# A change to a two-layer hybrid backbone on one core: where the weights of the passage between its layers, a block of adaLN, and the last head's sigmoids stand in the order of work

## The chip, the core and the metric

The kernel runs on one core of a Trainium2 chip. The time is the device time in microseconds of one execution of the program; several executions give a median. Engines are called TensorE (PE in rows), VectorE (DVE), ScalarE (ACT), GpSimd (POOL) and SyncE (SP, which issues the loads of the weights).

## What is computed

Two layers over 256 context and 512 latent tokens of width 1024. Each layer: RMS norm, a shift and scale from adaLN (a small matrix product with the condition c), a mixer of inner width 2048, and a residual with a gate from adaLN.

```python
# layer 0: HGRN2, 16 heads, forward and backward; layer 1: RG-LRU, 8 heads of 256, forward and backward
h = rms(x) * (1 + scale) + shift              # scale, shift, gate = adaLN(c)
# layer 0
q, v, zf, zb, g = split(h @ w_in)
o = scan(q, 1-f, log f, v)  both ways         # chunked; f = lb + (1-lb) sigmoid(z)
x += gate * ((rms(o) * silu(g)) @ w_out)
# layer 1
xb, g = split(h @ w_in); xb = conv4(xb)
r, i = sigmoid(xb @ w_a + b_a), sigmoid(xb @ w_x + b_x)
a = exp(-8 r softplus(-lam)); u = sqrt(1 - a*a) * (i * xb)
y = scan(a, u) both ways                      # h_t = a_t h_(t-1) + u_t
x += gate * ((y * silu(g)) @ w_out)
out = rms(x) for the latent tokens
```

## The kernel before

Products are kept in float32 precision with float32r operands: each matrix is held as a rounded part (hi) and a remainder (lo), and each product takes three matmuls, hi by hi, hi by lo and lo by hi (`mm3`, lines 307 to 313). A weight comes as one load of 512 KB into one of three raw buffers; ACT copies it to hi (line 129), DVE subtracts to lo (line 130). The class `Weights` keeps them in the order of first use: `get` loads and splits the weight asked for, loads some further ones, and, where `presplit` is set, splits the next one as well. `slots` gives a weight other buffers than the standard ones, and adaLN's weights are used raw. Where several instructions are ready, the framework orders each engine's queue by the order of the program and by priority; `high_priority(urgent)` puts the splits ahead of what stands around them. Each engine then runs its queue in order.

Layer 0 runs head by head. `hgrn(h)` holds seven levels of score products (`lv`), whose operands `kt`, `qt` and `QQ` come from ACT and DVE, then the states and the outputs. `head_in(h+1)`, the next head's input products, is interleaved as filler, and `out_item` adds the output product of two or three heads to x. adaLN's blocks for layer 1 run beside heads 9 to 14 as `side`: four weights of four loads each into `ada` (line 230), a copy `blk`, a transposing product `adat` and two adds (lines 235 to 246).

The passage (lines 722 to 743) is: the output product of head 15 (`o`, context tiles d = 0 to 7, then latent ones), with x updated by DVE (line 405), squares by ACT (`sq`) and their sums in three accumulators, one of which POOL adds (`acc`, line 289); after the last tile of a segment the norm's statistics, `rstd_of`: products `msh` with a vector of ones, the root `rh` on ACT, and `rbh`, its broadcast over the partitions by TensorE; then `hchunk`, which makes layer 1's input `h_hi` and `h_lo` through `scr`; and with each piece the first products of layer 1, `rc` for the context and `rl` for the latent tokens, of three weights.

Layer 1 runs 8 heads. `mixer(j)` first makes the gates (`gt`, evacuated by ACT's sigmoids into R and G), then T, A and R by tanh and exp, roots, DVE's scans and `yh`, `yl`; the next head's input products and the output product of the head before (`ro`) are the filler. ACT's functions come in sets that each need a table load, so `after` chains sigmoids, exps and roots. For the last head (j = 7) no next head is there: `held` adds the output products of heads 5 and 6 in eight accumulators, and the end is the output product of head 7, the sum of squares and the final norm.

## Time and profile before

| | us |
|---|---|
| median of 3 runs (lowest, highest) | 1578.45 (1577.46, 1580.52) |
| the profiled execution | 1582.77 |
| its span, first to last instruction | 1581.0 |
| TensorE busy | 1531.9 (97%) |
| DVE busy | 1194.8 (76%) |
| ACT busy | 902.2 (57%) |
| POOL busy | 11.5 (1%) |
| mean granted clock of TensorE | 0.986 |

The times of instructions below are those of the profiled execution, in microseconds from the start of its span. A busy TensorE is not one at its peak, since it also counts as busy at the lower clock. Releasers ("<-") are inferred from semaphores: the instruction that ended the wait.

### The profile page before, as it was taken

To read this page: it belongs to the slowest core of one execution; us is meant where nothing else is said; L and a number is where in the kernel's file an instruction comes from. 1 tells how busy PE (TensorE), PEld (TensorE's weight loads), DVE (VectorE), ACT (ScalarE), POOL (GpSimd) and SP (SyncE) were. 2 spreads that over 40 slices of the span, in tenths; PEclk is the share of its full clock that TensorE was granted. 3 is DMA by queue.
4 is the path that set the end of the run, shared out by engine and by line. 5 is a ranking of instruction groups with operands and counts; after the bars stand their busy time and mean duration, and the time that the engine had idled before them with its cause. 6 is when DMAs were issued, how large, how long until landed. Compare 5 with 4: busy or idle time off the path is not lost.

```text
span 1581.0 us, 33998 instructions
## 1 busy us (share of the span) xinstructions
PE 1531.9 (97%) x14740; PEld 1432.8 (91%) x14740; DVE 1194.8 (76%) x1848; ACT 902.2 (57%) x1422; POOL 11.5 (1%) x16
## 2 busy tenths in 40 slices
PE   5999999999999999999999999998999999999996
PEld 3899999999999999999999999987888888988985
DVE  4767678768867868867876776786758887897877
ACT  4554554555554554554545555654577577667783
POOL 0000000000000000000000000001000000000001
PEclk9999999999999999999999999998999999999998
DMA  8231211110211211223222131202212213222211
GB/s 327 81 121 55 95 55 41 55 55 28 82 41 42 68 42 54 81 68 98 69 92 80 55 111 65 95 15 67 67 54 81 81 54 94 80 68 73 75 40 53
DMA packets 33861, 116.80 MB, mean 74 GB/s; under 512 B 3632, under 2 KB 6064, under 8 KB 33712
## 3 DMA queue, kind: packets, MB, share of 16 engines
q1 hardware_dynamic: 32192, 113.26, 22.3%
q8 instruction: 116, 1.90, 0.5%
q10 hardware_dynamic: 1520, 1.37, 0.3%
q14 instruction: 33, 0.27, 0.0%
HBM read 112.52 MB, written 2.10 MB: 72 GB/s over the span
## 4 chain that ended last, share of the span: by engine, by line
PE 88%; DVE 5%; ACT 5%; issue 1%; DMA 1%; POOL 0%; POOLq 0%; ACTq 0%; DVEq 0%; SPq 0%
PE in L311 12%; PE in L312 11%; PE in L313 11%; PE v L381 9%; PE lv L460 4%; PE o L565 4%; PE r L313 3%; PE r L312 3%; PE r L311 3%; PE o L311 3%; PE o L313 3%; PE o L312 3%; PE gt L311 2%; PE gt L312 2%; PE gt L313 2%; PE U L533 2%
## 5 line engine op out<-in xcount | busy, mean ns | idle before, releaser
L311 PE MATMUL in<-h_hi,hi 128*128 128x384 f32 x1024 | 350.2, 343 | 3.4 <-ACT h_hi L304 2.7
L312 PE MATMUL in<-h_lo,hi 128*128 128x384 f32 x1024 | 345.7, 338 | 0.7 <-DVE h_lo L305 0.7
L313 PE MATMUL in<-h_hi,lo 128*128 128x384 f32 x1024 | 344.8, 337 | 0.0
L130 DVE TENSOR_TENSOR lo<-raw,hi 128x1024 fp32r<-128x1024 f32 x160 | 195.0, 1220 | 90.6 <-ACT hi L129 90.4
L129 ACT ACTIVATE hi<-raw 128x1024 fp32r<-128x1024 f32 x160 | 167.9, 1057 | 122.4 <-PE in L312 49.9
L311 PEld LDWEIGHTS in<-h_hi,hi 128*128 128x128 f32 x1024 | 192.8, 189 | 16.8 <-issue 9.9
L312 PEld LDWEIGHTS in<-h_lo,hi 128*128 128x128 f32 x1024 | 193.1, 189 | 3.0 <-issue 1.6
L313 PEld LDWEIGHTS in<-h_hi,lo 128*128 128x128 f32 x1024 | 192.8, 188 | 1.2 <-issue 0.8
L509 DVE TENSOR_TENSOR QQ<-QQ,T 128x768 f32<-128x768 f32 x112 | 117.6, 1050 | 20.7 <-ACT qt L491 20.5
L416 ACT ACTIVATE kt<-KK 128x768 f32<-128x768 f32 x112 | 102.5, 915 | 40.4 <-DVE KK L502 35.3
L502 DVE TENSOR_TENSOR KK<-KK,T 128x768 f32<-128x768 f32 x112 | 117.1, 1045 | 9.7 <-ACT kt L416 8.2
L313 PE MATMUL r<-h_hi,lo 128*128 128x512 f32 (+1 forms) x344 | 123.4, 359 | 0.3 <-DVE lo L130 0.3
L312 PE MATMUL r<-h_lo,hi 128*128 128x512 f32 (+1 forms) x344 | 123.1, 358 | 0.0
L311 PE MATMUL r<-h_hi,hi 128*128 128x512 f32 (+1 forms) x344 | 123.0, 357 | 0.0
L337 ACT ACTIVATE sg<-in 128x384 f32<-128x384 f32 x128 | 61.4, 482 | 100.1 <-PE in L313 100.0
L381 PE MATMUL v<-hi,h_hi 128*128 128x256 f32 x384 | 111.4, 290 | 0.0
L381 PE MATMUL v<-hi,h_lo 128*128 128x256 f32 x384 | 107.4, 280 | 0.0
L381 PE MATMUL v<-lo,h_hi 128*128 128x256 f32 x384 | 107.3, 279 | 0.0
L405 DVE SCALAR_TENSOR_TENSOR x<-o,ada,x 128x256 f32<-128x256 f32 (+1 forms) x184 | 82.4, 487 | 13.9 <-PE o L313 13.2
L588 DVE RECIPROCAL sq<-sq 128x384 f32<-128x384 f32 x30 | 76.4, 2548 | 21.1 <-ACT sq L582 21.1
L311 PE MATMUL gt<-xh,hi 128*128 128x384 f32 x256 | 86.5, 340 | 3.2 <-ACT G L838 2.9
L311 PE MATMUL o<-rhi,hi 128*128 128x384 f32 (+2 forms) x240 | 86.1, 360 | 2.8 <-DVE x L405 1.6
(208 smaller groups left out, 3268.0 us busy)
## 6 DMA issues: line engine op xcount, KB each, us to landing
raw<-in_hgw_dram SPq DMA_DIRECT2D x64, 512.0 KB, 3.6
raw<-in_ada_dram SPq DMA_DIRECT2D x48, 512.0 KB, 3.8
raw<-in_rgi_dram SPq DMA_DIRECT2D x32, 512.0 KB, 3.6
raw<-in_hgv_dram SPq DMA_DIRECT2D x16, 512.0 KB, 3.6
raw<-in_hgo_dram SPq DMA_DIRECT2D x16, 512.0 KB, 3.6
raw<-in_rgg_dram SPq DMA_DIRECT2D x16, 512.0 KB, 3.7
raw<-in_rgo_dram SPq DMA_DIRECT2D x16, 512.0 KB, 3.6
x<-in_x_dram SPq DMA_DIRECT2D x8, 384.0 KB, 5.8
```

The lines of the kernel that those rows point to most:

```text
L129: self.nc.scalar.activation(hi, r, AF.Copy)
L130: self.nc.vector.tensor_tensor(lo, r, hi.bitcast(F32), ALU.subtract)
L311: PE.matmul(ps, lhsT=wh, rhs=xh, start=first and i == 0, stop=False, skip_group_check=skip)
L312: PE.matmul(ps, lhsT=wh, rhs=xl, start=False, stop=False, skip_group_check=skip)
L313: PE.matmul(ps, lhsT=wl, rhs=xh, start=False, stop=last and i == n - 1, skip_group_check=skip)
L381: PE.matmul(ps, lhsT=xh[:, kk, t], rhs=w[:, k], start=part == 0 and k == 0 and i == 0 and c % 2 == 0, stop=part == 1 and k == 3 and i == 2 ...
L405: V.scalar_tensor_tensor(xs, ps[:, a - c.start:b - c.start], gate[:, d, 1 - j:2 - j], xs, ALU.mult, ALU.add)
L416: A.activation(view(kt, 0, [[2 * B, n], [B, 2], [1, B]]), view(KK, 0, [[2 * B, n], [NT + B, 2], [1, B]]), AF.Copy)
L460: PE.matmul(ps[w * g:w * g + w, w * c:w * c + w], lhsT=kt[:, o:o + w], rhs=rhs, start=c == 0, stop=c == NC - 1, skip_group_check=True, til ...
L502: V.tensor_tensor(kv, kv, view(T, 1, [[2, n], [m - 1, 2], [0, B]]), ALU.mult)
L509: V.tensor_tensor(qv, qv, view(T, m + 1, [[2, n], [-m - 1, 2], [0, B]]), ALU.mult)
L588: V.reciprocal(rs, rs)
```

## The change

- The output weight of head 15 and the first weight of layer 1 are asked for inside the output product of heads 12 to 14 (`later`), with buffers of their own in places that are free by then (two from layer 0's head buffers, one new pool `xwp`); two further weights of layer 1 are asked for ahead of the output product of head 15. The third accumulator moves from the S buffer to a V buffer.
- adaLN's last block for layer 1 (four weights) moves from beside head 14 into the passage: its weights behind the context's statistics, the rest behind the first of layer 1's gates. The context's statistics are called after the latent tile d = 4 instead of after the last context tile.
- In the last head of layer 1 the sigmoids get a high priority, the splits of the output weights lose theirs, and the output weights 13 and 14 go into the gate weights' buffers.

The diff:

```diff
--- before.py
+++ after.py
@@ -320,7 +320,7 @@
     p0 = lambda name, bufs=1: l0.enter_context(tc.tile_pool(name=name, bufs=bufs))
     qp, kdp, tp, ap_, sp, rp = p0("qp"), p0("kdp"), p0("tp"), p0("ap"), p0("sp"), p0("rp")
     qqp, kkp, gsp, ktp, qtp = p0("qqp", 2), p0("kkp", 2), p0("gsp", 2), p0("ktp", 3), p0("qtp", 2)
-    vp, tmp = p0("vp", 3), p0("tmp", 4)
+    vp, tmp, xwp = p0("vp", 3), p0("tmp", 4), p0("xwp")
     halves = (slice(0, HN), slice(HN, NT))
     st = [{} for _ in range(NH)]
     mtmp = tmp.tile([P, HN], F32, name="mtmp", tag="tmp")[:, :32 * NM]
@@ -388,8 +388,14 @@
                         A.activation(st[2 * g + u]["V"][:, 2 * b:2 * b + 2], src[:, :, P * u:P * u + P], AF.Copy)
                 yield 1300.0
 
+    later = {}
+
     def out_item(heads, accs=None, done=None):
-        ws = [wget("out", h) for h in heads]
+        ws = [later.pop("out") if "out" in later else wget("out", h) for h in heads]
+        if NH - 2 in heads:
+            W.presplit = False
+            later["out"] = wget("out", NH - 1)
+            later["rin"] = [wget("rin", 0, 0, 0)]
         gate = ada[0][:, 2]
         parts = segs if accs else halves
         order = [(d, i) for d in range(DK) for i in range(2)]
@@ -406,8 +412,8 @@
                                            ALU.mult, ALU.add)
             if accs:
                 sumsq(accs, THREE, lambda n: ktp.tile([P, NT], F32, name=n, tag="kt"), d, c)
-                if d == DK - 1:
-                    done(i)
+                if i and d > 3:
+                    done(d)
             yield 490.0 * len(heads)
 
     def gather(KK, kt, B):
@@ -612,6 +618,10 @@
         W.slots["ada", 0, i // 4, i % 4] = (rawp, "raw", 1024) if i in (10, 11) else wide[(i if i < 10 else i - 2) % 6]
     W.slots["v", 0, 0] = (wide[2], wide[0])
 
+    W.slots["out", NH - 1] = (wide[5], (xwp, "xw", 1024))
+    W.slots["rin", 0, 0, 0] = (wide[0], wide[1])
+    W.slots["rin", 0, 0, 1] = (wide[2], wide[0])
+
 
     acc0 = kdp.tile([P, NT], F32, name="acc0", tag="kd")
     for k in range(DK):
@@ -707,7 +717,7 @@
     def extra(h):
         if h in (1, 2):
             return [ada_block(0, 3 + h)]
-        return [ada_block(1, h - 10)] if h >= 10 else []
+        return [ada_block(1, h - 10)] if 10 <= h < NH - 1 else []
 
     for h in range(NH):
         if h == 0:
@@ -720,20 +730,27 @@
         interleave(hgrn(h, side), HW, chain_(fill), total)
         run_all(side)
     accs1 = [pl.tile([P, n], F32, name=f"acc1_{i}", tag=t)[:, :NT]
-             for i, (pl, t, n) in enumerate(((kdp, "kd", NT), (qp, "q", NT), (sp, "S", 2 * (NC - 1) * P)))]
+             for i, (pl, t, n) in enumerate(((kdp, "kd", NT), (qp, "q", NT), (vp, "V", NT)))]
     rs1 = []
 
-    def norm1(i):
+
+    later["rin"].extend(wget("rin", 0, x, e) for x, e in ((0, 1), (1, 0)))
+    side = ada_block(1, 5)
+
+    def norm1(d):
+        if d not in (4, DK - 1):
+            return
+        i = int(d > 4)
+        for _ in range(4 * i):
+            next(side)
         c = segs[i]
         rs1.extend(rstd_of([chunks(a, c) for a in accs1], ones_d, f"h1_{i}", ((c.stop - c.start) // P,)))
 
     run_all(out_item((NH - 1,), accs1, norm1))
 
 
-    W.presplit = False
-    wx = [wget("rin", 0, 0, e) for e in range(2)]
+    *wx, wg = later.pop("rin")
     first = [[(w, dtile(f"rc{e}")[:, :CTX]) for e, w in enumerate(wx)]]
-    wg = wget("rin", 0, 1, 0)
     first.append([(w, (dtile if e < 2 else atile)(f"rl{e}")) for e, w in enumerate(wx + [wg])])
     scr = [ktp.tile([P, NT], F32, name=f"scr1_{k}", tag="kt") for k in range(2)]
     for i, c in enumerate(segs):
@@ -752,6 +769,9 @@
     for j in range(RH):
         for jc in range(2):
             W.slots["gate", j, jc] = ((gwp, "gwh", 1024), (gwp, "gwl", 1024))
+
+    for i in (13, 14):
+        W.slots["rout", i] = ((gwp, "gwh", 1024), (gwp, "gwl", 1024))
     rt = [{} for _ in range(RH)]
     gate1 = ada[1][:, 2]
 
@@ -834,7 +854,7 @@
                         ps = atile(f"gt{j}_{d}_{jc}_{x}_{half}")[:, :HN]
                         mm3(ps, [(whi[:, d, x, i], wlo[:, d, x, i], s["xh"][:, i, c], s["xl"][:, i, c])
                                  for i in range(2)])
-                        with after("sqrt"):
+                        with after("sqrt"), tc.high_priority(600 if j == RH - 1 else 0):
                             turn["sig"] = A.activation(dst[:, c], ps, AF.Sigmoid, bias=prm_(b, col, 1), scale=1.0)
                     yield 1.0
                 V.tensor_tensor(Gt, Gt, s["xb"][:, jc], ALU.mult)
@@ -892,6 +912,7 @@
         for e in range(2):
             conv(0, e, i, first[i][e][1])
     g_evac(0, 0, first[1][2][1])
+    run_all(side)
     run_all(rin(0, ALL[1:2]))
     def part(ws, j, d, us, c):
         e = slice(P * d, P * d + P)
@@ -920,6 +941,7 @@
             phase(m, 12.0, rin(j + 1, ALL[:2]), 5200.0)
         else:
             phase(m, 8.0, None, 0.0)
+            W.urgent = 0
             run_all(held(j - 2, range(DK), []))
             phase(m, 20.0, held(j - 1, range(DK), []), 10400.0)
```

**TensorE's queue in the passage**, from the last latent tiles of head 15's output product on (`o15_d_1`; `hi`, `lo` with their number in the order of the weights; the last number of each name only counts). Before:

```order
L311 MATMUL o15_6_1_13008<-rhi15_12761,hi143_12472 128x512
L272 MATMUL rbh1_0_0_12961<-cst_78,rh1_0_12958 128x128 x2
L312 MATMUL o15_6_1_13008<-rlo15_12762,hi143_12472 128x512
L313 MATMUL o15_6_1_13008<-rhi15_12761,lo143_12473 128x512
L311 MATMUL o15_7_1_13016<-rhi15_12761,hi143_12472 128x512
L312 MATMUL o15_7_1_13016<-rlo15_12762,hi143_12472 128x512
L313 MATMUL o15_7_1_13016<-rhi15_12761,lo143_12473 128x512
L262 MATMUL msh1_1_13022<-cst_78,acc1_0_12884 128x1 x4
L311 MATMUL rc0_13051<-h_hi_94,hi144_12889 128x256
L262 MATMUL msh1_1_13022<-cst_78,acc1_1_12885 128x1 x4
L262 MATMUL msh1_1_13022<-cst_78,acc1_2_12886 128x1 x4
L311 MATMUL rc1_13052<-h_hi_94,hi145_13045 128x256
```

and now, from the tile d = 7:

```order
L313 MATMUL o15_7_1_12999<-rhi15_12738,lo139_12442 128x512
L272 MATMUL rbh1_0_0_12980<-cst_78,rh1_0_12977 128x128 x2
L230 MATMUL ada1_5_13005<-raw143_12868,sc_99 32x256 x4
L230 MATMUL ada1_5_13005<-raw144_12874,sc_99 32x256 x4
L230 MATMUL ada1_5_13005<-raw145_13006,sc_99 32x256 x4
L262 MATMUL msh1_1_13032<-cst_78,acc1_0_12861 128x1 x4
L311 MATMUL rc0_13053<-h_hi_94,hi140_12447 128x256
L262 MATMUL msh1_1_13032<-cst_78,acc1_1_12862 128x1 x4
L262 MATMUL msh1_1_13032<-cst_78,acc1_2_12863 128x1 x4
L311 MATMUL rc1_13054<-h_hi_94,hi141_12864 128x256
L230 MATMUL ada1_5_13005<-raw146_13012,sc_99 32x256 x4
L272 MATMUL rbh1_1_0_13048<-cst_78,rh1_1_13045 128x128 x4
```

The context's `rbh` stands behind the last latent tile instead of inside the one before, `msh` of the latents is preceded by three of the four weights of adaLN, and the fourth stands between the first `rc` of the second weight and the latents' `rbh`.

**DVE's queue where head 15's output operand `rlo15` is made.** Before:

```order
L405 SCALAR_TENSOR_TENSOR x1_81<-o12_7_0_12861,ada0_96,x1_81 128x256
L405 SCALAR_TENSOR_TENSOR x1_81<-o12_7_0_12861,ada0_96,x1_81 128x128
L130 TENSOR_TENSOR lo143_12473<-raw143_12464,hi143_12472 128x1024
L130 TENSOR_TENSOR lo144_12890<-raw144_12470,hi144_12889 128x1024
L599 TENSOR_TENSOR rlo15_12762<-gs15_12335,rhi15_12761 128x256
L604 TENSOR_TENSOR rlo15_12762<-gs15_12335,rhi15_12761 128x8x64
L405 SCALAR_TENSOR_TENSOR x1_81<-o12_7_1_12873,ada0_96,x1_81 128x384
L405 SCALAR_TENSOR_TENSOR x1_81<-o15_0_0_12893,ada0_96,x1_81 128x256
L405 SCALAR_TENSOR_TENSOR x1_81<-o15_1_0_12899,ada0_96,x1_81 128x256
L405 SCALAR_TENSOR_TENSOR x1_81<-o15_2_0_12907,ada0_96,x1_81 128x256
L130 TENSOR_TENSOR lo145_13046<-raw145_12887,hi145_13045 128x1024
L405 SCALAR_TENSOR_TENSOR x1_81<-o15_3_0_12915,ada0_96,x1_81 128x256
```

and now:

```order
L601 TENSOR_TENSOR gs15_12304<-gs15_12304,rbv1_0_12830 128x512
L411 SCALAR_TENSOR_TENSOR x1_81<-o12_7_0_12838,ada0_96,x1_81 128x256
L411 SCALAR_TENSOR_TENSOR x1_81<-o12_7_0_12838,ada0_96,x1_81 128x128
L130 TENSOR_TENSOR lo142_12871<-raw142_12451,hi142_12870 128x1024
L605 TENSOR_TENSOR rlo15_12739<-gs15_12304,rhi15_12738 128x256
L610 TENSOR_TENSOR rlo15_12739<-gs15_12304,rhi15_12738 128x8x64
L411 SCALAR_TENSOR_TENSOR x1_81<-o12_7_1_12850,ada0_96,x1_81 128x384
L411 SCALAR_TENSOR_TENSOR x1_81<-o15_0_0_12876,ada0_96,x1_81 128x256
L411 SCALAR_TENSOR_TENSOR x1_81<-o15_1_0_12882,ada0_96,x1_81 128x256
L411 SCALAR_TENSOR_TENSOR x1_81<-o15_2_0_12890,ada0_96,x1_81 128x256
```

One split stands ahead of `rlo15` instead of two, and none among the x of head 15; the output weight of head 15 (number 139 now, 143 before) is split earlier.

**ACT's queue at the last head of layer 1** (`gg7` the gate branch, `R7` and `G7` sigmoids, `yh6` the output of head 6). Before:

```order
L773 ACTIVATE gg7_16480<-r7_1_0_1_16446 128x512
L773 ACTIVATE gg7_16480<-r7_1_1_1_16496 128x512
L838 ACTIVATE R7_0_0_16529<-gt7_0_0_0_0_16532,prm_76 128x384
L838 ACTIVATE R7_0_0_16529<-gt7_0_0_0_1_16540,prm_76 128x384
L129 ACTIVATE hi203_16681<-raw203_16601 128x1024
L129 ACTIVATE hi204_16687<-raw204_16679 128x1024
L872 ACTIVATE yh6_16412<-T6_1_0_16184 128x512
L838 ACTIVATE G7_0_0_16530<-gt7_0_0_1_0_16548,prm_76 128x384
L838 ACTIVATE G7_0_0_16530<-gt7_0_0_1_1_16556,prm_76 128x384
```

and now:

```order
L793 ACTIVATE gg7_16484<-r7_1_0_1_16450 128x512
L858 ACTIVATE R7_0_0_16533<-gt7_0_0_0_0_16536,prm_76 128x384
L858 ACTIVATE R7_0_0_16533<-gt7_0_0_0_1_16544,prm_76 128x384
L793 ACTIVATE gg7_16484<-r7_1_1_1_16500 128x512
L858 ACTIVATE G7_0_0_16534<-gt7_0_0_1_0_16552,prm_76 128x384
L129 ACTIVATE hi203_16685<-raw203_16605 128x1024
L858 ACTIVATE G7_0_0_16534<-gt7_0_0_1_1_16560,prm_76 128x384
L858 ACTIVATE R7_1_0_16569<-gt7_1_0_0_0_16572,prm_76 128x384
L892 ACTIVATE yh6_16416<-T6_1_0_16188 128x512
L858 ACTIVATE R7_1_0_16569<-gt7_1_0_0_1_16580,prm_76 128x384
L129 ACTIVATE hi204_16691<-raw204_16683 128x1024
```

The sigmoids of `G7_0_0` that stood behind two splits and `yh6` now stand ahead of `yh6`, with one split between their halves; `yh6` and the second split stand among the sigmoids of the next gate.

## Rows read from the trace of the kernel before

**Rows 1.** The page, part 1: engine, busy time and its share of the span, instructions.

```profile
PE 1531.9 (97%) x14740; PEld 1432.8 (91%) x14740; DVE 1194.8 (76%) x1848; ACT 902.2 (57%) x1422; POOL 11.5 (1%) x16
```

**Rows 2.** Windows of the passage: stretch, length, busy times by engine, PEclk, DMA.

```profile
1074.00:1084.00 10.00, 5.77 (x34) 4.36 (x32) 9.30 (x17) 7.25 (x13) 2.97 (x3) 1.00 0.46 149
1084.00:1094.60 10.60, 10.60 (x34) 8.96 (x35) 5.08 (x9) 4.06 (x8) 1.81 (x2) 0.52 0.03 10
1094.60:1101.00 6.40, 3.74 (x28) 3.09 (x26) 5.66 (x9) 3.64 (x6) 2.04 (x2) 1.00 0.29 78
1101.00:1108.00 7.00, 7.00 (x35) 7.00 (x36) 4.92 (x12) 2.98 (x6) 0.00 (x0) 0.51 0.26 78
1108.00:1127.00 19.00, 17.83 (x90) 14.57 (x90) 15.33 (x28) 7.30 (x13) 0.00 (x0) 1.00 0.09 28
```

**Rows 3.** Waits of TensorE, 1060 to 1160: us in total, times, longest.

```profile
PE rc L311 <- ACT h_hi L304: 1.8, 1, 1.8
PE o L311 <- DVE x L405: 1.6, 2, 0.9
PE msh L262 <- POOL acc L289: 1.5, 2, 0.9
PE o L311 <- DVE lo L130: 1.2, 1, 1.2
PE rl L312 <- DVE h_lo L305: 1.2, 1, 1.2
PE o L312 <- DVE rlo L599: 0.9, 1, 0.9
```

**Rows 4.** Timeline of ACT: start, length, line, operation, count [idle before <-releaser].

```profile
1073.99 2.00 ACT L129 ACTIVATE hi<-raw 128x1024 fp32r<-128x1024 f32 x2 [2.67 <-PE o L312]
1075.91 0.40 ACT L598 ACTIVATE rhi<-gs 128x256 fp32r<-128x256 f32 x1
...
1091.34 0.26 ACT L265 ACTIVATE rh<-msh,epst 128x2 f32<-128x2 f32 x1 [5.29 <-PE msh L262]
```

**Rows 5.** Timeline of DVE, the splits of weights in the passage.

```profile
1075.09 2.36 DVE L130 TENSOR_TENSOR lo<-raw,hi 128x1024 fp32r<-128x1024 f32 x2 [0.70 <-ACT hi L129]
...
1080.47 1.26 DVE L130 TENSOR_TENSOR lo<-raw,hi 128x1024 fp32r<-128x1024 f32 x1
...
1096.78 1.23 DVE L130 TENSOR_TENSOR lo<-raw,hi 128x1024 fp32r<-128x1024 f32 x1
```

**Rows 6.** TensorE in heads 14 and 15: ada, a wait, and the window of 1018 to 1055.

```profile
1001.69 0.64 PE L230 MATMUL ada<-raw,sc 128*32 128x256 f32 x8
...
1020.67 0.95 PE L240 MATMUL adat<-cst,blk 128*128 128x2 f32 x8
...
PE lv L460 <- ACT qt L416: 2.5, 2, 1.6
...
1018.00:1055.00 37.00, 33.92 (x519) 30.79 (x518) 36.31 (x58) 22.85 (x36) 0.00 (x0) 1.00 0.10 30
```

**Rows 7.** The page, part 6: DMA issues, KB each, median us to landing.

```profile
raw<-in_ada_dram SPq DMA_DIRECT2D x48, 512.0 KB, 3.8
```

**Rows 8.** Timeline of TensorE in the tail, the two long waits.

```profile
1514.15 0.66 PE L311 MATMUL gt<-xh,hi 128*128 128x384 f32 x1 [2.87 <-ACT G L838]
...
1557.46 0.98 PE L311 MATMUL ro<-yh,hi 128*128 128x256 f32 x6 [4.07 <-ACT yh L872]
```

**Rows 9.** Window of the tail behind the first of them.

```profile
1514.20:1517.50 3.30, 3.30 (x11) 3.30 (x12) 3.30 (x5) 1.89 (x4) 0.00 (x0) 0.50 0.00 0
```

**Rows 10.** Timeline of ACT in the tail.

```profile
1508.73 2.02 ACT L129 ACTIVATE hi<-raw 128x1024 fp32r<-128x1024 f32 x2
1513.00 0.63 ACT L872 ACTIVATE yh<-T 128x512 fp32r<-128x512 f32 x1 [2.24 <-DVE T L871]
...
1545.67 0.63 ACT L872 ACTIVATE yh<-T 128x512 fp32r<-128x512 f32 x1 [0.81 <-DVE T L871]
```

**Rows 11.** Timeline of DVE in the tail.

```profile
1537.47 2.35 DVE L130 TENSOR_TENSOR lo<-raw,hi 128x1024 fp32r<-128x1024 f32 x2
```

## The prediction

> **What bounds the kernel now.** I read the page first: TensorE is busy 97% of the span [rows 1], so a change that keeps its work can win only where it waits or runs at its lower clock. Next the windows: they show where that is. [...] Last the waits of TensorE: in the passage they end on DVE's weight split (lo), rlo, x, POOL's acc, ACT's h_hi and DVE's h_lo [rows 3], all of them small engines' work queued behind something else. The same reading of the tail finds one wait of 2.87 us for a sigmoid (G), 3.3 us at the lower clock behind it, and one of 4.07 us for yh [rows 8, 9]. Between the two, in layer 1, TensorE is the bound, so what is won in the passage should reach the end.
>
> The profiled execution took 1582.77 us (span 1581.0 and 1.77 around it), 4.3 above the median of the runs, 1578.45. I sum against the trace and take the sum off the median. A measurement of this kernel tells about 0.2% (3.2 us) from no change.
>
> **Passage, waits.** They sum to 1.8 + 1.6 + 1.5 + 1.2 + 1.2 + 0.9 = 8.2 us [rows 3].
> - *lo and rlo, 2.1 us.* Today ACT runs two hi's (2.00 us) and only then rhi, and DVE two lo's (2.36 us) and only then rlo [rows 4, 5]. The change leaves one of each ahead, the other weights being split in head 15. rhi comes 1.0 us and rlo 1.2 us sooner: 1.0 us of waiting is left.
> - *x, 1.6 us.* One of the two waits is DVE's third lo (1.26 us at 1080.47 [rows 5]) between the x's. It leaves the place; 0.7 is left.
> - *acc, 1.5 us.* The first msh now stands behind five latent tiles, so POOL's acc is old by then. The second stands behind ada's matmuls, and ACT starts the latents' squares sooner: today it sits 5.29 us on the context's root, because TensorE comes late to msh [rows 4]. None left.
> - *h_hi, 1.8 us.* Today a lo (1.23 us at 1096.78 [rows 5]) precedes the first scr; it goes, and ada's matmuls lie in front. 0.3 left.
> - *h_lo, 1.2 us.* DVE's own pace, with two more lo's moved among the latents' scr's. Matmuls of the next weight are now interleaved there as filler; I count nothing won. 1.2 left.
> - *New: ada's fourth weight.* Three raw buffers hold ada's four weights, so the fourth's DMA starts only after TensorE has used the first, and an ada weight takes 3.8 us from issue to landing [rows 7]. Between them on TensorE's queue stand two ada weights (2 x 0.6 us [rows 6]), 12 msh columns and two rc's, some 2.5 us by these rows. The wait lies between 0 (where the rc's wait anyway) and 1.3, and it holds rbh of the latents behind it. I take 0.7, the middle.
>
> Left are 1.0 + 0.7 + 0.3 + 1.2 + 0.7 = 3.9 us: 4.3 won (2.5 to 5.5).
>
> **Passage, work added.** adaLN's block: four weights at 0.64 us a group, 0.57 by their pitch, and the transposing matmuls, 0.95, 0.8 by their pitch [rows 6]: **3.1 us of TensorE** more here. Its evacuation by ACT and two small adds stand behind work that has slack.
>
> **Passage, clock.** The two stretches lose 10.6 x 0.48 + 7.0 x 0.49 = 5.1 + 3.4 = 8.5 us [rows 2]. Each follows a stretch in which TensorE idled 4.2 of 10 and 2.7 of 6.4 us. After the change I get about 1.7 in the first and under 1 in the second. A stretch with idle of this order is in the trace: 1018 to 1055 holds 3.1 us of idle, and the clock stays at 1.00 [rows 6]. So I take both as gone: **8.5 won** (3.4 if only the second goes, 0 at worst).
>
> [...] No single wait ahead of the first drop is longer than 1.2 us [rows 3]. [...]
>
> **Heads 14 and 15.** The 3.1 us of ada leave. Part of it comes back as waiting: there lv already waits 2.5 us for qt, and DVE is busy 36.3 of 37 us from 1018 to 1055 [rows 6], so TensorE gets there sooner only to wait. I give back 1.4 of the 3.1. One lo more (1.2 us) also falls into that full stretch of DVE, and delays qt. Net **0.5 won**; bounds 2.0 won (lo in slack) and 0.9 lost (all of ada's time given back, lo partly hidden).
>
> **Tail.** Today ACT does gg twice, R twice, then two hi's (2.02 us), then yh, which waits 2.24 us for DVE, and only behind it the G that TensorE needs [rows 10]. Now one hi stands between G's halves, and all of this G ahead of yh.
> - The wait of 2.87 us [rows 8] goes, and the 3.3 us at clock 0.50 behind it [rows 9], worth 1.65. Two ro matmuls (0.5) fall behind the last gt. Against that: a hi (1.0 us) stands ahead of the last G, in time that ACT mostly waits, 0.8; and small waits of TensorE for the hi's between the sigmoids, 0.4. Last gt and G: 3.8 sooner.
> - Two lo's of the output weights (2.35 us [rows 11]) leave DVE's queue ahead of the scan, and two hi's leave ACT's. What comes next is late then: yh had 0.81 of waiting [rows 10], and behind it now stand an exp and the table load ahead of the roots. Of the 2.35 I count 1.5.
> - The last lo still stands among the last scans: nothing. The last ro's start on a cold clock as today: nothing.
>
> **5.3 won** (3.0 to 6.5).
>
> **Sum.** 4.3 - 3.1 + 8.5 + 0.5 + 5.3 = 15.5 us. The trace would go to 1567.3, the median to 1578.45 - 15.5 = **1563.0 us**.
>
> **Rivals.**
> - *One half-clock stretch stays.* rlo's and x's waits remain close together at the start, and the clock falls at the same place: 5.1 back, 1568.1. For it: TensorE still waits 1.7 us within some 5. Against: 1018 to 1055. If both stay, whatever the waits do, it is 1571.5; against it, each stands right behind a cluster of waits and at no other place of the passage. [...]
> - *The tail stands still.* G is sooner, but DVE's chain of scans sets yh all the same, and the hi's between the sigmoids hold TensorE as long as yh did. Then only the passage counts: 1568.3. Against: the chain starts from the last G, and nothing on it grows but one hi.
> - *DVE becomes the bound and the result is slower.* From the first scr on, TensorE has 7.0 us at the lower clock and 17.8 at the upper up to 1127 [rows 2], 21 us of work at full speed; DVE is busy 20.3 us in it, and two more lo's come in. At full speed TensorE could run dry again and again, and the clock fall for the whole phase: each us of work then costs one more. From 15.5 us of the 21 on, nothing is left of the gain; all of it gives 1563.0 + 21 = 1584. Against: a slow TensorE runs dry no more, and the two stretches of the trace ended after 10.6 and 7.0 us of work; and there is filler now.
> - *The change does not do what it says.* The order of instructions as shown with the change excludes it for the places named; no chance of its own.
>
> **How the numbers follow.** Forecast (both stretches gone, tail won; its own range 1559 to 1567) 0.50; one stretch stays 0.16; both stay 0.06; tail stands still 0.13; a stretch stays and the tail stands still, 1573.4 to 1576.8, 0.06; DVE's bound costs all or more 0.09, of which 0.05 slower and 0.04 within 0.2%. Faster by over 0.2% needs under 1575.3: 0.50 + 0.16 + 0.06 + 0.13 and half of the next 0.06, 0.88; within 0.2% the other half and 0.04, 0.07; slower 0.05. The range reaches from the best bounds (head 2.0, tail 6.5, waits 5.5: 19.4 won, some 1559) to the first two rivals with poor bounds, 1573; it leaves out about 2 in 10.
>
> **What would show it.** Right: granted clock 1.00 throughout the passage; TensorE's first o of head 15 waits about 1 us instead of 2.1; no wait for POOL's acc; at most 1.3 us between the last rc ahead of ada's fourth weight and that weight; no wait of gt for G over 1 us; the last yh some 5 us closer to the last xb of head 7. Wrong: a stretch at 0.5 in the passage (first rival), a wait for ada's raw of 3 us or more, waits of rc and rl for h_lo that add to more than 4 us (third), or heads 14 and 15 longer than before by over 1 us.

## The result, and the profile after

The changed kernel takes 1568.52 us (median of 6 executions, 1568.14 to 1570.48); the kernel before, run beside it, 1578.33 (6 executions, 1577.22 to 1580.52). The ratio is 0.9939, interval 0.9929 to 0.9949: 9.8 us, or 0.6%, faster. The forecast of 1563.0 had the direction, and the range holds the time, but 15.5 us were forecast and 9.8 came.

The profiled execution of the changed kernel took 1568.14 us (span 1566.3), 0.4 under its median and the fastest of the six. The profiled one of before took 1582.77, 4.3 over its own. The two traces thus differ by 14.6 us and the medians by 9.8. The first question is where each trace gained; the second is why the executions gained less.

The page of the changed kernel, part 1 (engine, busy time, share, instructions), answers to [rows 1]: the work is the same, and TensorE needs 6.8 us less for it.

```profile
PE 1525.1 (97%) x14740; PEld 1428.1 (91%) x14740; DVE 1194.7 (76%) x1848; ACT 901.8 (58%) x1422; POOL 11.1 (1%) x16
```

Windows of the changed kernel (stretch, length, busy times of PE, PEld, DVE, ACT, POOL, granted clock, DMA share and GB/s): the five stretches of [rows 2], then one in head 14 and one in the tail.

```profile
1074.00:1084.00 10.00, 8.48 (x54) 7.53 (x53) 7.88 (x17) 5.05 (x10) 1.68 (x3) 1.00 0.16 53
1084.00:1094.60 10.60, 10.49 (x83) 8.65 (x81) 9.22 (x16) 5.86 (x12) 4.76 (x4) 1.00 0.22 73
1094.60:1101.00 6.40, 6.40 (x54) 5.70 (x54) 5.41 (x13) 5.67 (x11) 0.00 (x0) 1.00 0.60 209
1101.00:1108.00 7.00, 7.00 (x46) 6.27 (x45) 6.92 (x15) 3.80 (x7) 0.00 (x0) 1.00 0.21 63
1108.00:1127.00 19.00, 19.00 (x84) 15.39 (x83) 14.88 (x23) 9.12 (x12) 0.00 (x0) 1.00 0.28 88
1001.90:1005.30 3.40, 3.40 (x29) 3.28 (x25) 0.96 (x1) 1.53 (x4) 0.00 (x0) 0.50 0.00 0
1541.20:1548.10 6.90, 6.46 (x29) 6.24 (x30) 4.66 (x10) 3.41 (x9) 2.19 (x3) 0.51 0.00 0
```

In this execution both half-clock stretches of the passage (0.52 and 0.51 in [rows 2]) read 1.00, and TensorE is busy 8.48 of the first 10 us instead of 5.77. Two stretches at 0.50 stand elsewhere: 3.4 us in head 14, where there was none, and 6.9 us at the start of the last ro, where before had 3.4.

Waits of TensorE in the changed kernel (us in total, times, longest): three rows of 1060 to 1160, which answer to [rows 3], and below the gap the tail, which answers to [rows 8].

```profile
PE o L312 <- DVE rlo L605: 0.7, 1, 0.7
PE o L311 <- DVE x L411: 0.6, 1, 0.6
PE o L311 <- ACT rhi L604: 0.2, 1, 0.2
...
PE ro L311 <- ACT yh L892: 3.3, 1, 3.3
PE msf L262 <- POOL acc L289: 1.8, 1, 1.8
```

The waits for lo, acc, h_hi and h_lo, 5.7 us in [rows 3], are gone; what is left in the passage is 1.5 us of 8.2 (the 0.2 for rhi is new). In the tail, no gt waits for G; the last ro waits 3.3 for yh instead of 4.07. The wait of msf belongs to the final norm and is nearly the same in before (1.9).

TensorE's timeline of the changed kernel (start, length, line, operation, count, and in brackets the idle time before with its releaser), in head 14, head 15 and the passage:

```profile
1000.50 0.61 PE L466 MATMUL lv<-qt,kt 128*32 128x32 f32 x46 [1.32 <-ACT qt L497]
...
1035.85 0.44 PE L311 MATMUL o<-r,hi 128*128 128x384 f32 x1 [1.10 <-ACT r L609]
...
1039.88 0.44 PE L311 MATMUL o<-rhi,hi 128*128 128x384 f32 x1 [0.76 <-DVE gs L341]
...
1078.02 0.62 PE L311 MATMUL o<-rhi,hi 128*128 128x256 f32 x3 [0.24 <-ACT rhi L604]
1079.31 0.39 PE L312 MATMUL o<-rlo,hi 128*128 128x256 f32 x1 [0.67 <-DVE rlo L605]
...
1090.47 1.50 PE L230 MATMUL ada<-raw,sc 128*32 128x256 f32 x24
1091.90 1.05 PE L262 MATMUL msh<-cst,acc 128*128 128x1 f32 x8
...
1095.28 0.64 PE L230 MATMUL ada<-raw,sc 128*32 128x256 f32 x8
```

The first o of head 15's 256 columns starts at 1078.02. The same matmul of before starts at 1076.36, though 3.1 us of ada stand no longer ahead of it. Ada's first three weights run in one piece at 1090.47, and the fourth at 1095.28 without a wait.

Matched matmul by matmul, the two traces agree up to head 14. **Heads 14 and 15 lose 1.7 us** (1076.36 to 1078.02). In layer 1 the changed kernel runs 10.05 us ahead, so **the passage wins 11.7**. At the last head's gt it is 15.0 ahead, at the last yh 15.8, at the end of the span 14.7: **the tail wins 4.65**. From trace to trace, the sum of 15.5 was within 1 us; part of that is luck, since the two traces stand at opposite ends of their kernels' spreads.

### The profile page after: what moved, and what is told of

It reads as the page before. It is cut to its first block, busy times and chain, and to the rows that moved or that the text cites. A ratio compares the mean times of both kernels' runs of the same rounds, so it can differ in the third digit from the quotient of the medians.

```text
span 1566.3 us, 33993 instructions
## 1 busy us (share of the span) xinstructions
PE 1525.1 (97%) x14740; PEld 1428.1 (91%) x14740; DVE 1194.7 (76%) x1848; ACT 901.8 (58%) x1422; POOL 11.1 (1%) x16
## 3 DMA queue, kind: packets, MB, share of 16 engines
q1 hardware_dynamic: 32192, 113.26, 22.7%
## 4 chain that ended last, share of the span: by engine, by line
PE 91%; DVE 4%; ACT 4%; issue 1%; DMA 0%; POOL 0%; POOLq 0%; ACTq 0%; DVEq 0%
PE in L311 11%; PE in L312 11%; PE in L313 11%; PE v L381 9%; PE r L313 4%; PE r L312 4%; PE r L311 4%; PE lv L466 4%; PE o L571 4%; PE gt L311 3%; PE o L311 3%; PE gt L312 3%; PE gt L313 3%; PE o L312 3%; PE o L313 3%; PE U L539 2%
## 5 line engine op out<-in xcount | busy, mean ns | idle before, releaser
L313 PE MATMUL gt<-xh,lo 128*128 128x384 f32 x256 | 85.8, 336 | 0.0
```

What stands on the lines that cost most here:

```text
L313: PE.matmul(ps, lhsT=wl, rhs=xh, start=False, stop=last and i == n - 1, skip_group_check=skip)
```

## The experiments

Medians are those of the kernel and of before in the same group of runs. Three kernels had a single execution, for their trace.

### How far one execution of the kernel before stands from another

The kernel before, unchanged.

> The kernel before, unchanged, for the spread of its executions. Theory A (the clock differs from execution to execution): the profiled execution shown ahead of the prediction was 4.3 us over the median because its half-clock stretches in the passage were long; the executions here differ in granted clock, by about 1.6 us for each 0.001 of it (0.001 of a 1580 us span), most at 0.988 to 0.990, and another trace of it shows less than 17 us at half clock in the passage. Rival B: the clock reads 0.986 in all of them, and the 4.3 us lie in some other place.

It took 1579.05 (11 executions, 1578.28 to 1583.46), beside 1578.88 (26 executions, 1576.88 to 1582.80). The ratio is 1.0009, interval 1.0001 to 1.0018: even the same kernel against itself shows 0.1%. Of the 48 executions of before in two groups of runs, those with a mean granted clock of 0.985 took 1581.6 on average (11 of them), 0.987 took 1578.9 (15), and 0.990 took 1577.7 (6). The spread of some 6 us goes in the main with the clock.

Both traces of before are from its slow end. The second, of 1582.67 us, windows (columns as above):

```profile
1083.70:1094.00 10.30, 10.30 (x31) 8.66 (x32) 4.84 (x9) 4.04 (x8) 1.43 (x2) 0.50 0.03 11
...
1100.80:1107.60 6.80, 6.80 (x33) 6.80 (x34) 4.62 (x11) 2.78 (x6) 0.00 (x0) 0.50 0.28 80
```

These are the same two stretches as in [rows 2], so the expectation that another trace of before would show less of them did not come true. What stands is the spread: the trace that the clock term was read from is no median execution.

### The changed kernel again

> The changed kernel unchanged, beside the three below on the same chip, for the spread of its executions. Theory A: its executions differ by 2 to 6 us, with the granted clock (0.985 to 0.991); the median is 1568 to 1571, and its lowest is near 1568. Rival B: all stay within 2.5 us as in the first six, and the median is 1568.5.

1569.80 (6 executions, 1568.04 to 1570.71) against 1578.47; ratio 0.9943, interval 0.9932 to 0.9955. Its profiled execution is another than the first one. Windows:

```profile
1034.00:1038.20 4.20, 2.59 (x55) 1.59 (x55) 4.20 (x6) 2.19 (x3) 0.00 (x0) 1.00 0.13 26
1038.20:1041.60 3.40, 3.20 (x13) 2.77 (x13) 3.40 (x6) 0.84 (x1) 0.00 (x0) 0.50 0.79 269
...
1085.00:1092.80 7.80, 7.69 (x69) 6.29 (x67) 7.32 (x13) 4.75 (x9) 3.87 (x3) 1.00 0.24 77
1092.80:1099.60 6.80, 6.80 (x35) 5.77 (x36) 3.46 (x9) 3.76 (x8) 0.00 (x0) 0.50 0.64 223
```

The same program has 6.8 us at the lower level in the passage this time, though TensorE was busy 7.69 of the 7.8 us before it and its waits of the passage are the small ones of after. So the stretch in the passage is not gone. It comes in this execution and, as a table further below shows, in all traces of a kernel with this passage but the first. In head 14 the clock stayed at 1.00 here; the 3.4 us stand in head 15 instead, behind 4.2 us in which TensorE worked 2.59 and DVE all the time. The first o of 256 columns starts at 1076.67, 0.3 us later than before instead of 1.7.

A time can be split with the mean granted clock of its execution: time x (1 - clock) is half of the time spent at the lower level, which reads 0.50 to 0.52 in the windows, and time x clock the rest. The clock is given to 0.001, which is 1.6 us in one execution, so only means over several say anything. The split is an estimate, since it takes every lower-clock microsecond as half lost, also where TensorE waited in it.

| kernel, executions | mean us | mean clock | lost to the clock | rest |
|---|---|---|---|---|
| before, 48 | 1579.2 | 0.9873 | 20.1 | 1559.1 |
| after, 12 | 1569.3 | 0.9893 | 16.9 | 1552.4 |
| difference | 9.9 | | 3.2 | 6.7 |
| forecast | 15.5 | | 10.15 | 5.35 |
| the profiled pair | 14.6 | | 8.1 | 6.5 |

### The tail alone

Before, with the tail's three edits:

```diff
+    for i in (13, 14):
+        W.slots["rout", i] = ((gwp, "gwh", 1024), (gwp, "gwl", 1024))
...
-                        with after("sqrt"):
+                        with after("sqrt"), tc.high_priority(600 if j == RH - 1 else 0):
...
+            W.urgent = 0
```

> The kernel before with the third part of the change alone (sigmoids of the last head first, output weights 13 and 14 in the gates' buffers). Theory A (the parts add up): 4.7 us under the kernel before, 1573.6, the amount by which the two traces part between the last head and the end; the passage reads as in the kernel before. Rival B: without the passage the tail gives under 2 us, since the wait for yh stays the last to end.

1575.53 (12 executions) against 1578.88; ratio 0.9982, interval 0.9972 to 0.9991: 3.3 us, between the two theories (4.7 and under 2). Beside the first trace of before, the trace is 2.6 us ahead in layer 1, 6.9 at the last gt of the last head and 7.4 at the last yh, so the tail wins 4.3 us up to that gt and 4.8 up to yh. Waits of TensorE in its tail:

```profile
PE ro L311 <- ACT yh L874: 3.3, 1, 3.3
PE msf L262 <- POOL acc L289: 1.8, 1, 1.8
```

G's wait is gone and yh's is 3.3, as in the changed kernel: the tail's edits work by themselves.

### The passage alone

The changed kernel without these three edits.

```diff
-    for i in (13, 14):
-        W.slots["rout", i] = ((gwp, "gwh", 1024), (gwp, "gwl", 1024))
...
-                        with after("sqrt"), tc.high_priority(600 if j == RH - 1 else 0):
+                        with after("sqrt"):
...
-            W.urgent = 0
```

> The changed kernel without its third part (the tail as before). Theory A: the median gains what is left of 9.8, 5.1 us: 1573.2; no half-clock stretch in the passage, one of 3.4 us in head 14. Rival B (the tail adds nothing of its own): 1568.5 as the changed kernel.

1574.62 (9 executions, 1567.52 to 1576.62) against 1578.88; ratio 0.9964, interval 0.9949 to 0.9978: 4.3 us. The executions form two groups: five of 1574.6 to 1576.6 at clock 0.985 to 0.988, and four of 1567.5 to 1571.1 at 0.991 to 0.992. The profiled one, 1576.25, is of the slower group. Its windows:

```profile
1089.50:1094.90 5.40, 5.29 (x53) 4.11 (x51) 5.00 (x8) 3.20 (x6) 2.58 (x2) 1.00 0.38 129
1094.90:1101.70 6.80, 6.80 (x35) 5.77 (x36) 3.70 (x9) 4.00 (x8) 0.00 (x0) 0.50 0.55 206
```

Again 6.8 us at 0.50 behind a stretch in which TensorE worked 5.29 of 5.4 us. The expectation had none in the passage; the 3.4 us that it had in head 14 came. Alone the passage gives 4.3 in the median and the tail 3.3; their sum of 7.6 is a little under the 8.7 to 9.8 of both together.

### Ada's block back in heads 14 and 15

```diff
-        return [ada_block(1, h - 10)] if 10 <= h < NH - 1 else []
+        return [ada_block(1, h - 10)] if h >= 10 else []
...
-    side = ada_block(1, 5)
...
-        for _ in range(4 * i):
-            next(side)
...
-    run_all(side)
```

> The changed kernel with adaLN's last block beside head 14 again. Theory A (the block was filler that head 14 needed): the waits of lv for qt in head 14 (1.3 us now) fall under 0.5 and the half-clock stretch there goes, 1.7 us won up to head 15's output product; the passage loses 3.1 us of work and gets a wait of 1 to 1.5 us for h_hi in its place: 1565 to 1567 in all. Rival B (the block keeps TensorE's clock in the passage): its wait for h_hi grows to 1.8 us or more, a half-clock stretch follows, and the time is 1570 or more.

1571.70 (5 executions); ratio 0.9951, interval 0.9939 to 0.9963. Neither theory holds: the time is above the first's 1565 to 1567, and h_hi's wait, which was to grow to 1.8 us by the second, is 0.4. Waits of TensorE, 995 to 1160:

```profile
PE o L313 <- DVE lo L130: 1.9, 1, 1.9
PE msh L262 <- POOL acc L289: 1.2, 1, 1.2
PE lv L466 <- ACT qt L422: 0.9, 1, 0.9
...
PE rc L311 <- ACT h_hi L304: 0.4, 1, 0.4
```

With ada back, acc (1.2) and h_hi (0.4) hold TensorE in the passage, where the changed kernel has no wait for either; lv waits 0.9 for qt, not 2.7 (1.4 and 1.3, at two lines), and o waits 1.9 for a lo. The o of 256 columns starts at 1076.51, with ada's 3.1 us ahead of it; without them it came at 1076.67 and 1078.02. On the whole kernel ada's place is worth 1.9 to 3.2 us by the medians, with intervals that overlap.

### Ada back, and the latents' statistics as before

The kernel above, and:

```diff
-                if i and d > 3:
-                    done(d)
+                if d == DK - 1:
+                    done(i)
```

and `norm1` takes the segment, as before.

> The changed kernel with adaLN's last block beside head 14 and the context's statistics where they stood before: of the passage only the earlier splits are left. Theory A (lo and hi in front of rlo and scr were the larger part of the waits): the waits for lo, rlo and h_hi are as in the changed kernel, the waits of msh for POOL's acc come back (1.5 us), and with them more half clock: 1572 to 1574.5. Rival B (the splits alone give all): 1571.7 or less, as with the statistics moved.

1570.55 (5 executions); ratio 0.9951, interval 0.9939 to 0.9963, the same as above, so the second theory holds (1571.7 or less). Calling the context's statistics after the latent tile d = 4, without ada between, shows no gain. In the passage x waits 0.7, rlo 0.7, h_hi 0.7, acc 1.2 and rhi 0.2: 3.5 us of the 8.2 are left where neither ada nor the statistics are moved, so most of the waiting that goes, goes with the splits.

### The splits later in head 15's output product

DVE's timeline shows what precedes the 0.76 us wait for gs, in the kernel before and, below the gap, in the changed one:

```profile
1035.48 1.21 DVE L130 TENSOR_TENSOR lo<-raw,hi 128x1024 fp32r<-128x1024 f32 x1
1036.60 0.61 DVE L341 SCALAR_TENSOR_TENSOR gs<-in,prm,sg 128x384 f32<-128x384 f32 x1
...
1036.95 2.34 DVE L130 TENSOR_TENSOR lo<-raw,hi 128x1024 fp32r<-128x1024 f32 x2
1039.22 0.60 DVE L341 SCALAR_TENSOR_TENSOR gs<-in,prm,sg 128x384 f32<-128x384 f32 x1
```

Two lo's stand ahead of gs, in the stretch where DVE has no slack [rows 6], where before had one: head 14's output weight stood there already, and head 15's is new. The lo of layer 1's first weight, asked for at the same place, comes only at 1062.11, behind that stretch. The edit asks for the two weights within the output product instead of at its start:

```diff
-        ws = [later.pop("out") if "out" in later else wget("out", h) for h in heads]
-        if NH - 2 in heads:
-            W.presplit = False
-            later["out"] = wget("out", NH - 1)
-            later["rin"] = [wget("rin", 0, 0, 0)]
+        ws = []
+        for h in heads:
+            if h == NH - 2:
+                W.presplit = False
+            ws.append(later.pop("out") if "out" in later else wget("out", h))
...
+            if (NH - 2 in heads, i, d) == (True, 0, 6):
+                later["out"] = wget("out", NH - 1)
+            if (NH - 2 in heads, i, d) == (True, 0, 7):
+                later["rin"] = [wget("rin", 0, 0, 0)]
```

> The changed kernel, with head 15's output weight and layer 1's first weight asked for at the tiles d = 6 and d = 7 of the output product of heads 12 to 14 instead of ahead of it, so that their hi and lo come behind the stretch in which DVE is full. Theory A (these two splits delay gs and qt in head 15): the waits of 0.8 us for gs and 1.1 for r there shrink, head 15's output product starts 1 to 1.5 us sooner, the rest of the trace is as in the changed kernel: 1.0 to 1.5 us under it. Rival B: DVE is as full later, rlo of head 15 comes later instead, and the time is that of the changed kernel within 1 us.

1567.18 (5 executions, 1566.14 to 1568.47); ratio 0.9928, interval 0.9916 to 0.9940, 2.6 us under the changed kernel beside it. Waits of TensorE, 995 to 1160:

```profile
PE o L311 <- ACT r L613: 1.1, 1, 1.1
PE lv L470 <- ACT qt L426: 0.9, 1, 0.9
PE lv L470 <- DVE QQ L519: 0.9, 2, 0.5
```

No row for gs is left; the wait for ACT's r stays. In the medians it is 2.6 us. How much of it is the path, the next run and a table behind it tell.

### The same, with ada back

The later splits, and the edit of ada above.

> As the one before, and adaLN's last block beside head 14 again. Theory A: 1 to 2 us under the kernel with only the block put back (1571.7 there), since its wait of 1.9 us of the output product for lo in head 15 goes: about 1570; it stays above the changed kernel with later splits by the 2 to 3 us by which the block's place differed. Rival B: the block's place makes no difference beyond the clock of single executions, and it equals the changed kernel with later splits within 1 us.

1568.74 (5 executions); ratio 0.9934, interval 0.9922 to 0.9946. It is 1.6 slower than with ada in the passage, with intervals that overlap. Its trace has lv waiting 2.5 us for qt, acc 1.3 and 10.2 us at the lower clock in the passage. Both pairs of medians point to ada standing better in the passage; in the means of these two kernels it is 0.9 us (1568.24 and 1567.35). Whether there is a gain, the runs do not settle.

What the heads 14 and 15 gained can be read without the medians: from the first ada matmul at about 915 us, ahead of them in every trace, to the first o of 256 columns behind them (three of the kernels follow below).

| traces | splits | ada | lower clock in the heads | us |
|---|---|---|---|---|
| before, two | none here | here | none | 160.7 |
| after; passage alone | at the product's start | moved | 3.4 us in head 14 | 162.4, 162.4 |
| after again | at the product's start | moved | 3.4 us in head 15 | 161.1 |
| ada back | at the product's start | here | none | 161.1 |
| the same, statistics as before | at the product's start | here | 3.4 us in head 15 | 160.9 |
| later splits; two without homes | later | moved | none | 159.7, 159.7, 159.8 |
| later splits without priority; without mark | later | moved | 3.4 us in head 14 | 161.3, 161.3 |
| later splits, ada back | later | here | none | 159.5 |

Three differences stand out. With the same stretch in head 14, asking for the splits at the start of the product costs **1.1 us** over the later place (162.4 to 161.3); with ada here and no stretch it is 1.6 (161.1 to 159.5). The stretch in head 14 costs **1.6 us** (161.3 to 159.7); that in head 15 shows no cost (160.9 with it, 161.1 without), TensorE waiting there anyway. And ada's leaving wins **nothing**: 159.5 with it here, 159.7 without. All of its 3.1 us come back as waiting.

### Which of the tail's edits does it

Three kernels, each with the later splits and one of the edits taken back: the sigmoids' priority, the gates' homes, the urgent mark.

```diff
-                        with after("sqrt"), tc.high_priority(600 if j == RH - 1 else 0):
+                        with after("sqrt"), tc.high_priority(0):
```

> The kernel with later splits (the sixth run), the sigmoids of the last head at their usual priority; the buffers of output weights 13 and 14 and the splits' lost priority stay. One trace, read from the last head on. Theory A (the priority is what brings G ahead of yh): the wait of gt for G comes back with 1.8 to 2.9 us, and the part from the last head to the end is 2 to 3.5 us longer than in the sixth run. Rival B (the splits without priority make room for G anyway): no wait of gt over 0.5 us and under 0.5 us lost.

```diff
-    for i in (13, 14):
-        W.slots["rout", i] = ((gwp, "gwh", 1024), (gwp, "gwl", 1024))
```

> The sixth run without the gates' buffers for output weights 13 and 14, so that their splits wait for standard buffers and stand behind the first tanh of the second pair; priority as changed. One trace, read from the last head on. Theory A (two lo's, 2.3 us, are again on DVE's chain ahead of the second pair's roots): the last yh comes 1.5 to 2.5 us later, and hi no longer stands ahead of the last G, 0.8 us sooner: 0.7 to 1.7 us longer in all. Rival B: yh's wait hides them, within 0.5 us.

```diff
-            W.urgent = 0
```

> The sixth run with the splits' priority kept in the tail (it stays at 100): the last weight's lo moves from the last scans to those of the first pair. One trace, read from the last head on. Theory A (DVE's chain of the last pair is the end's bound, and the first pair's has slack of 1.4 us at yh): the last yh comes up to 1.1 us sooner. Rival B: what the last pair wins, the roots of the second pair lose, since hi and lo stand ahead of them: within 0.4 us.

The single times are 1570.02, 1563.76 and 1568.96, which differences of 1 us can't be read from; the traces can. I measure from ACT's table load for the roots of head 6 (1.28 us at 1489.80 in the changed kernel), ahead of the last head's sigmoids, to the last yh: 51.17 us with all three edits, 52.67 without the priority, 51.63 without the homes, 51.55 without the mark (before: 55.6). The priority is worth 1.5, the others 0.4 to 0.5 each, where the first theories had 1.5 to 2.5 for the homes and a loss of up to 1.1 by the mark. G's wait, which was to come back without the priority, comes back in none of the three (gt waits 0.3 us for R there, and not at all in the others); without all three edits, in the passage alone, it is 1.8 us. So the priority gains its 1.5 us, but none of the three edits is needed by itself for that wait to go. Behind yh it is the other way round: from the last yh to the end the kernel with all three takes 24.04 and the one without homes 22.69 (24.6 without the priority, 25.1 without the mark). Waits of TensorE in the tail without the priority:

```profile
PE ro L311 <- ACT yh L896: 4.3, 1, 4.3
```

and without the homes:

```profile
PE ro L311 <- ACT yh L894: 1.5, 1, 1.5
PE ro L313 <- DVE lo L130: 1.5, 1, 1.5
```

Without the homes the last weights are split late, so TensorE waits in the midst of the ro's for a lo and then less for yh; its clock stayed at 1.00 at the last ro.

### The later splits without the gates' homes, timed

> The tenth run's kernel, in rounds: the changed kernel with the two early splits asked for later and without the gates' buffers for output weights. Theory A (a single wait of 3.3 us ahead of the last ro's brings half clock there, two of 1.5 do not): its traces show no half clock from the last yh to the last xb, 22.7 us from the last yh to the end instead of 24.0, and the median is 1565 to 1566.5, 1 us or more under the sixth run's 1567.2. Rival B (the single trace of the tenth run had luck with the clock): the median is 1567 to 1568.

**1564.91 us** (5 executions, 1564.08 to 1566.65) against 1578.98; ratio **0.9912**, interval 0.9899 to 0.9926, as the first theory has it. It beats both kernels: its interval lies apart from that of the changed kernel (0.9929 to 0.9949), though it overlaps with that of the version that keeps the homes. Windows, one in the passage and two from the last scans on:

```profile
1093.00:1096.40 3.40, 3.40 (x22) 3.02 (x15) 2.66 (x7) 2.67 (x6) 0.00 (x0) 0.51 0.75 254
1536.00:1540.00 4.00, 3.60 (x16) 2.63 (x15) 3.93 (x5) 0.00 (x0) 0.00 (x0) 1.00 0.00 0
1540.00:1546.00 6.00, 4.89 (x40) 4.89 (x41) 4.65 (x12) 3.70 (x9) 2.01 (x3) 1.00 0.00 0
```

The passage still has 3.4 us at the lower level. The last ro runs at 1.00 behind two waits of 1.5 us, where that of the changed kernel ran 6.9 us at 0.51 behind one of 3.3. From the last yh to the end this takes 22.7 us; the version with homes took 24.04 with 3.4 us at the lower level, and the changed kernel 25.32 with 6.8 in its first trace and 24.00 with 3.4 in its second: 1.3 us for each 3.4. (In the two traces of before it is 0.6: 24.20 with 3.4 and 24.79 with 6.8.) On average this kernel loses 11.6 us to the clock, the version with homes 14.7 and the changed one 16.9; the rest is 1553.7 against 1552.6 and 1552.4.

How long each trace shows the lower level (0.50), in us:

| traces | passage | last ro |
|---|---|---|
| before, two | 17.1, 17.1 | 3.4, 6.8 |
| the tail alone | 13.7 | 3.4 |
| after, after again | 0, 6.8 | 6.8, 3.4 |
| the passage alone | 6.8 | 6.8 |
| ada back; the same, statistics as before | 3.4; 6.8 | 6.8; 6.8 |
| later splits; the same, ada back | 3.4; 10.2 | 3.4; 3.4 |
| later splits without priority; without mark | 3.4; 3.4 | 6.8; 6.8 |
| later splits without homes, two | 3.4, 3.4 | 0, 0 |

Behind a single last wait of 3.3 to 4.3 us for yh all twelve traces have 3.4 or 6.8 us at the lower level; the only two without are the two with that wait split. Which of 3.4 and 6.8 comes differs between executions of one kernel.

## Why the prediction was right in its direction and 5.5 us too good

**The step that failed is "Passage, clock", 8.5 won, taken off the median.** The stretches were there, and by the estimate of half they cost 8.5 us in that trace; in the profiled pair it is 8.1 us over the whole kernel. But over all executions 3.2 us are won by the clock where the sum had 10.15 with the tail's 1.65. That is a net figure, in which the new 3.4 us in head 14 or 15 count against the passage. Two things are behind it. First, the trace of before stands 4.3 us over its median and at the low end of its clocks (0.986, of 0.985 to 0.990), and a term of it was taken off the median as if every execution had it in full. The only trace near a median with before's passage, the tail alone, has 13.7 us at the lower level there and not 17.1. Second, the changed kernel doesn't stay at 1.00: of eight traces with its passage only the first has no stretch there, five have 3.4 us and two 6.8, all from 1091.7 to 1094.9 on. From the means of these traces (16.0 us with before's passage, 3.8 with the changed one) the passage wins some 6.1 us of clock, an estimate, and not 8.5; two of the three traces with before's passage were taken some 4 us above the median, so it may be less.

The first rival, that one stretch stays (1568.1), was thus the nearest, though its number fits the measured 1568.5 in part by luck: it gave back 5.1 us, and a stretch of 3.4 to 6.8 us costs 1.7 to 3.4 by the same estimate; the rest was lost elsewhere. It named the start of the passage, with rlo's and x's waits, as the place. There the clock stayed up (1.00 from 1074 to 1084 in the first trace); it fell near 1093, some 15 us later, behind ada's, msh's and rbh's small matmuls, in a stretch where TensorE by the trace is busy over 97%.

That the clock stays at 1.00 once less idle stands ahead was my estimate, and of the eight traces one bears it out. No long gap and hardly an idle stands ahead of the 6.8 us in the second trace of the changed kernel (7.69 of 7.8 us busy). The 3.4 us in head 15 stand behind short waits (2.59 of 4.2 us busy). In the tail, 6.8 or 3.4 us at the lower level stand behind one wait of 3.3 to 4.3, none behind two of 1.5.

**Passage, waits: 4.3 forecast, 6.7 measured.** lo and rlo, x, acc came out as worked out (0.9, 0.6 and 0 us left, for 1.0, 0.7 and 0). Ada's fourth weight caused no wait (0.7 taken, the middle of 0 to 1.3), h_hi left none (0.3) and h_lo none (1.2): the next weight's matmuls do cover h_lo's pace, which I had counted at nothing.

**Work added: 3.1 forecast.** The four weights stand in the passage with 1.50 + 0.64 us by their own rows, ada's three weights in one piece being shorter than three groups apart (3 x 0.57); with the transposes' 0.95 it is 3.1.

**Heads 14 and 15: 0.5 won forecast, 0.3 to 1.7 lost.** The bounds were 2.0 won and 0.9 lost. All of ada's 3.1 us came back, not 1.4: ACT's r (1.10), gs (0.76) and qt hold TensorE where ada had filled the time. The one lo more ahead of gs, with the splits asked for there, costs 1.1 us, much as the sum had it (1.2). And the first trace has 3.4 us at the lower clock in head 14, 1.6 us, which no part of the sum had. I took the window of 1018 to 1055 [rows 6] as proof that the clock stays up with this much idle, and then took out work that filled these heads. "Longer than before by over 1 us" was named as a sign of error, and it is what the first trace shows.

**Tail: 5.3 forecast, 4.65 in the traces, 3.3 in the medians of the tail alone.** At the last head's gt 4.95 is won (3.8 forecast) and up to the last yh 0.8 more (1.5 forecast). Then 1.1 is lost, as the last ro's stay 6.8 us at the lower level in this trace, not 3.4. That is the execution more than the change: the second trace of before has 6.8 there and the second of the changed kernel 3.4, so the "nothing" that was counted for the last ro's start, at the lower clock as before, stands. Of the 1.5 forecast up to yh, which was to come from the two lo's out of DVE's queue, the gates' homes give 0.5 by the kernel without them, and they cost 1.35 behind yh.

**The rivals of the other side** are out. DVE did not become the bound: no wait for h_lo or h_hi is left, and from 1108 to 1127 TensorE is busy all 19 us with DVE at 14.88. The tail did not stand still.

What stays open is why the clock falls near 1093. Two windows, of the first trace of the changed kernel, where it does not fall, and, below the gap, of the kernel with ada back and the statistics as before, where it does:

```profile
1085.70:1093.50 7.80, 7.69 (x66) 6.16 (x64) 7.16 (x13) 4.74 (x9) 3.85 (x3) 1.00 0.15 41
...
1084.90:1092.70 7.80, 5.91 (x36) 4.76 (x35) 5.85 (x11) 4.45 (x9) 3.86 (x3) 1.00 0.00 0
1092.70:1096.10 3.40, 3.40 (x18) 3.40 (x18) 0.57 (x2) 0.00 (x0) 0.00 (x0) 0.51 0.00 0
```

TensorE's 7.69 busy us of 7.8 are the same in the first trace as ahead of the fall in the second, so the busy share does not tell them apart. And ada's matmuls are not needed for the fall: it comes in all three kernels with ada back too (at 1094.0, 1092.7 and 1090.5), there behind waits for acc and h_hi. msh's and rbh's small matmuls stand close ahead of the fall in all of these traces, but no kernel was made with them elsewhere, so the cause stays open.

## What to carry to other kernels

A term of the sum that rests on the granted clock should be read from several executions: list time and mean clock of each, and see where the traced one stands among them, before its half-clock stretches are taken off a median. Work that is moved sooner is best put where its engine has slack: the same two splits, one of which had stood in the full stretch, were worth 1.1 us on the path a few tiles later in the same product. And one long wait in the tail cost more here than two short ones of nearly the same sum: with earlier homes for two weights the last wait was 3.3 us in one piece, with 3.4 us at the lower level behind it and 24.04 us from the last yh to the end; with two waits of 1.5 us none, and 22.69.

## What was not expected of the hardware

The clock falls at different places in executions of one program: the changed kernel showed 3.4 us at 0.50 in head 14 and none in the passage in one execution, 3.4 us in head 15 and 6.8 us in the passage in the next. It fell for 6.8 us behind 7.8 us in which TensorE was busy for 7.69, and not in the first execution, which was as busy there (7.69 of 7.8 us, at 1.00).

An execution of before at 0.985 takes 3.9 us longer than one at 0.990, though by the estimate of half it would be 0.005 x 1580 = 7.9. Some of the lost time may be covered by waits that a faster TensorE would have had; no run shows where.
